# Eight buffers of split weights at eight different offsets within 512 bytes

## The chip, the cores and the metric

The kernel runs on one core of one Trainium2 chip. The metric is the time of one execution on the device in microseconds (us); where several runs are shown, it is their median. The engines are named as in the profile: PE is TensorE (PEld its weight loads), DVE is VectorE, ACT is ScalarE, POOL is GpSimd, SP is SyncE, which here only issues DMAs.

## What is computed

A trunk of two layers over 512 tokens of 1024 channels, in float32. Both layers have a token mixer and then a channel mixer with gated units, each between two RMS norms:

```python
# layer 0: retention heads and 2-D neighbourhood attention, side by side
proj = hn @ w_in
...
return jnp.concatenate([ret_out, na_out], axis=-1) @ w_out

# layer 1: bidirectional state-space mixer (SSD), 32 heads in 4 groups
proj = hn @ w_in
z, xbc, dt_raw = jnp.split(proj, [SSD_INNER, SSD_INNER + SSD_XBC], axis=-1)
xbc = jax.nn.silu(depthwise_conv_centered(xbc, conv_w, conv_b))
...
return y.astype(hn.dtype) @ w_out

# after either: up projection, convolution of width 3, gate, down projection
u = depthwise_conv_centered(hn @ w_up, conv_w, conv_b)
gate, val = jnp.split(u, 2, axis=-1)
return (jax.nn.gelu(gate, approximate=True) * val) @ w_down
```

## The kernel before

Nearly all of the work is in the weight matrices, which lie in HBM in tiles of 128 x 1024 float32. TensorE multiplies them as float32r. To keep the precision of float32, both sides of a product are split into a high part, which is the value rounded by a copy, and a low part, which is what remains. One product then takes three matmuls into the same PSUM tile (`mm3`, lines 116 to 118): high by high, low by high and high by low.

A weight tile goes through three steps. The SP queue loads it into `wst`, one of 3 buffers of 4096 bytes a partition. ScalarE copies it to `whi` (line 107) and VectorE subtracts to `wlo` (line 108), 4 buffers each:

```python
self.wst = pool("wst", 3)
self.whi = pool("whi", 4)
self.wlo = pool("wlo", 4)
```

TensorE then reads slices of 128 columns (512 bytes) of them as the stationary operand, while 512 or 256 columns of the activations `xh`, `xl` stream past (`proj_fm`), or it streams 512 columns of `whi` and `wlo` past slices of the activations (`down_tm`, the down projections, the output projections). In the rows of the profile, `mm<-xh,whi` streams `xh` over a slice of `whi`, and `mm<-whi,ab1h` streams `whi` over a slice of `ab1h`.

The feed-forward layers use Strassen's scheme: `up_strassen` makes its combined weights with `parts`, `down_strassen` with `weights`, whose activations are the tiles `axh`, `axl`, `ab1h` and `ab1l`. `mixer1` is the state-space layer. It computes the step widths first (`steps`, from a weight tile of 512 columns that is read in slices of 64), then per head a decay matrix (`head`: a row `pb` is loaded by a DMA on ACT's queue, 8 ScalarE operations on it at line 1101, an exponential into `e`), and per pair of heads the products and sums into `y`.

The order of each engine's work comes from the order of the code and from priorities (`high_priority`), with semaphores that the framework sets. The pools lie one behind the other in each partition. With `whi` and `wlo` buffers of 4096 bytes every one of the eight begins at a multiple of 512 bytes, and so do the streams `wst`, `xh`, `xl`, `H` and most work tiles. Three unused tiles do that too: "pad" in its own pool of 48 floats, and "gap" and "pad" of 32 floats each in the pool `few` of `mixer1`. Exceptions are the residual `x`, whose rows are 4224 bytes apart, and some tiles of the feed-forward layer such as `G`, `V` and `wx`, which begin at byte 480 of a block.

Of the kernel before, what the change touches and what calls it, by code (L numbers as in the profile page):

```python
# [8 lines left out]
F32 = mybir.dt.float32  # L9
R32 = mybir.dt.float32r  # L10
# [7 lines left out]
P = 128  # L18
# [12 lines left out]
class Env:  # L31
# [32 lines left out]
    def operands(self):  # L64

        self.xh, self.xl = (self.res.tile([P, KD, S], R32, name=n, tag=n) for n in ("xh", "xl"))

    def chore(self, n=1):

        for _ in range(min(n, len(self.chores))):  # L70
            self.together([self.chores.pop(0)()], [self.product])
# [9 lines left out]
    def wunit(self, src, parts=None, st=None, behind=None, low_behind=None):  # L81

        if st is None:
            st = self.wload(src)
        halves = slice(0, 512), slice(512, 1024)
        if parts is None:
            hi, lo = self.whi.tile([P, 1024], R32, name="whi"), self.wlo.tile([P, 1024], R32, name="wlo")
            with self.tc.high_priority(60):  # L90
                self.split(hi, lo, st, behind, low_behind)
            return [(hi[:, c], lo[:, c]) for c in halves]
        with nullcontext() if behind else self.tc.high_priority(60):
            for j, c in enumerate(halves):
                self.split(parts[j], parts[j + 2], st[:, c], behind)
        return [(parts[j], parts[j + 2]) for j in range(2)]
# [181 lines left out]
def down_strassen(E, big, pool, w, ts, H, first, g_post, done):  # L278
# [9 lines left out]
    def stage(i, u, cols):  # L288
        st = pool.tile([P, 1024], F32, name="wx", tag="k3") if k0[0] % 4 == 3 else E.wst.tile([P, 1024], F32, name="wst")
        k0[0] += 1  # L290
        nc.sync.dma_start(st[:, :cols], quarters(*i)[u])
        return st[:, :cols]

    def weights(i, u, extra=None):
        cols = 1024 if u < HK // 2 else 512
        st = stage(i, u, cols)
        if extra is None:
            hi, lo = E.whi.tile([P, 1024], R32, name="whi"), E.wlo.tile([P, 1024], R32, name="wlo")
        else:
            hi, lo = extra[:, :1024], extra[:, 1024:]  # L300
        with tc.high_priority(150):
            E.split(hi[:, :cols], lo[:, :cols], st)
        return [(hi[:, c:c + 512], lo[:, c:c + 512]) for c in range(0, cols, 512)]
# [34 lines left out]
    for i, (src, bank) in enumerate(seq):  # L338
# [12 lines left out]
        if last:  # L351
            ex = {4: big.tile([P, 2048], R32, name="x1", tag="s3"), 5: big.tile([P, 2048], R32, name="x2", tag="e2")}
            ws = [weights(src, u, ex.get(u)) for u in range(HK // 2 + 1)]
            for t in range(2):
                for u, x in enumerate(ws):
                    if (t, u) == (0, 1):
                        E.operands()
                    if u == 1:
                        E.finish(f"t{t}", st, done)
                    mms(t, x, u)  # L360
                E.post_half(st, 2 + t, 1, bank[t], g_post, sign=-1.0)
                E.finish(f"x{2 + t} s{2 + t}", st, done)
            continue
        for uu in ((0,), (1,), (2,), (3,), (4, 5)):
            ws = [(weights(src, u), u) for u in uu]
            for t in range(2):
                for x, u in ws:
                    mms(t, x, u)
            if uu == (1,):
                nxt = prepare(i + 1)  # L370
# [58 lines left out]
def up_strassen(E, w_up, f, X, G, V):  # L429

    nc, tc = E.nc, E.tc
    low, high = slice(0, HW), slice(HW, S)

    def load(pool, name, s, h):
        st = pool.tile([P, 1024], F32, name=name)
        nc.sync.dma_start(st.rearrange("p (f c) -> p f c", f=2),
                          w_up[s, f:f + 2, :, h * 512:h * 512 + 512].rearrange("f p c -> p f c"))
        return st  # L440

    def parts(st):
        hi, lo = E.whi.tile([P, 1024], R32, name="whi"), E.wlo.tile([P, 1024], R32, name="wlo")
        E.split(hi, lo, st)
        return hi, lo

    add = lambda o, x, y: nc.vector.tensor_tensor(o, x, y, op=ALU.add)
    q = {}

    def weights(i):  # L450
        with tc.high_priority(60):
            if i == 0:
                q[11] = load(E.wst, "wst", 0, 0)
                return parts(q[11])
            if i == 1:
                q[12], q[22] = load(E.wst, "wst", 1, 0), load(E.wst, "wst", 1, 1)
                add(q[11], q[11], q[12])
                add(q[12], q[12], q[22])
                return parts(q[12])
            if i == 2:  # L460
                q[0] = E.gain.tile([P, D], F32, name="gain")
                add(q[0], q[11], q[22])
                return parts(q[0])
            if i == 3:
                q[21] = load(E.gain, "gain", 0, 1)
                add(q[0], q[0], q[21])
                return parts(q[0])
            return parts(q[{4: 11, 5: 21, 6: 22}[i]])

    a = [E.mm.tile([P, S], F32, name="mm") for _ in range(2)]  # L470
    b, d = ([E.px.tile([P, S], F32, name="pu", tag="px") for _ in range(2)] for _ in range(2))
    order = ("A11", a), ("S3", b), ("S2", a), ("A22", b), ("R1", a), ("A12", d), ("S4", a)
    for i, (n, bank) in enumerate(order):
        hi, lo = weights(i)
        more = i in (2, 3, 4, 6)
        for j in range(2):
            for k in range(4):
                c = slice(j * 512 + k * P, j * 512 + k * P + P)
                E.mm3(bank[j][:, :HW], hi[:, c], lo[:, c], X[n][0][:, k], X[n][1][:, k], not more and k == 0, k == 3, more)
        if i == 4:  # L480
            t = E.tmp.tile([P, 2, HW], F32, name="w5", tag="tmp")
        for j in range(2):
            r = bank[j][:, :HW]
            if i in (3, 5):
                o = G[:, j, low if i == 3 else high]
                add(o, r, o)
            else:
                o = t[:, j] if i == 4 else {0: G[:, j, high], 1: V[:, j, low], 2: G[:, j, low], 6: V[:, j, high]}[i]
                nc.scalar.copy(o, r)
        if i == 4:  # L490
            add(V[:, :, low], t, V[:, :, low])
        if i in (2, 5):
            E.chore(2)
# [406 lines left out]
def mixer1(E, w_dt, w_fm, cw, dtc, cols, mask, w_out, g_post_row, done, ahead):  # L900
# [8 lines left out]
    with ExitStack() as ctx:  # L909
# [1 line left out]
        one, two, four = pool("m1", 1), pool("m1b", 2), pool("m1d", 4)  # L911

        few = pool("m1s", 1)
        few.tile([P, 32], F32, name="gap")
        few.tile([P, 32], F32, name="pad")

        cwt = few.tile([P, NG, 6, 6], F32, name="cwt")
# [18 lines left out]
        def steps():  # L936

            st = E.wst.tile([P, 512], F32, name="wst")
            nc.sync.dma_start(st, w_dt)
            wh = E.whi.tile([P, 512], R32, name="whi")  # L940
            wl = E.wlo.tile([P, 512], R32, name="wlo")
            E.split(wh, wl, st)
            ps = E.mm.tile([P, S], F32, name="mm")
            for k in range(KD):
# [286 lines left out]
        for i in range(3):  # L1231
            project(gs[0], i, p0[i])
        steps()
        ys, last, hrows, three = pool("m1y", 2), pool("m1f", 1), pool("m1p", 3), pool("m1e", 5)
        for _ in range(3):
# [49 lines left out]
def trunk(tc, x, norms, ab, ssd, ffns, out):  # L1285

    nc = tc.nc
    with ExitStack() as ctx:
# [39 lines left out]
        def ahead(w):  # L1328
            up = ffns[1][0]
            w1.extend((E.wunit(up[0, 0]), E.wunit(up[1, 0], low_behind=w), E.wload(up[0, 1])))  # L1330

        mixer1(E, *ssd, norms[1, 1], then(norms[1, 2]), ahead)
        E.chores = sums(E, ffns[1][2], ts[1])
        ffn(E, *ffns[1], ts[1], norms[1, 3], store, w1)
# [121 lines left out]
```

## Time and profile before

| | |
|---|---|
| time, median of 3 runs | 1370.81 us (1370.14 to 1371.52) |
| profiled execution | 1372.97 us, span of its instructions 1371.2 us |
| PE, PEld busy | 1344.3 us (98%), 1136.2 us (83%) |
| DVE, ACT, POOL busy | 1088.5 us (79%), 815.2 us (59%), 111.5 us (8%) |
| granted TensorE clock | 0.998 |
| DMA | 229.90 MB, mean 168 GB/s |

The profile is one execution. The span goes from its first to its last instruction; the profiled time also holds what lies around it. A record of a matmul runs from its start to its modelled end, so records of consecutive matmuls overlap: the pace is read from one start to the next. The chain of work is followed back from the last instruction to whatever released each step; a share of it is time that set the end. A group is all instructions of one line with the same tiles, with its count, busy time, the mean of one in ns, and the idle time of its engine before them.

### The profile page before, as it was taken

How to read it: one execution, taken by the hardware profiler on the slowest of the kernel's cores; microseconds unless marked ns; L12 is line 12 of the kernel's file. 1: busy time of each engine (PE TensorE's matmuls, PEld its weight loads, DVE VectorE, ACT ScalarE, POOL GpSimd, SP SyncE). 2: the span in 40 equal slices, each digit the busy share in tenths (PEclk: the TensorE clock that was granted, in tenths of full speed). 3: DMA queues.
4: the chain of work that ended last, by engine and by line, in shares of the span. 5: the costliest groups of instructions: out<-in, count | busy, mean ns of one | idle time of the engine just before them, and what ended most of it. 6: DMA issues, size and time to landing. Idle time of an engine off the chain costs nothing.

```text
span 1371.2 us, 19491 instructions
## 1 busy us (share of the span) xinstructions
PE 1344.3 (98%) x7352; PEld 1136.2 (83%) x7352; DVE 1088.5 (79%) x1524; ACT 815.2 (59%) x1345; POOL 111.5 (8%) x130
## 2 busy tenths in 40 slices
PE   7999999999999999999999999999999999999997
PEld 6877777798999888888778788787878899998886
DVE  7368878696768889697878876898789877888876
ACT  5356667453554566664878778477555455556563
POOL 1001110100111100020000110000010001110000
PEclk9999999999999999999999999999999999999999
DMA  7443232126779946654566455174433678994654
GB/s 298 144 138 99 89 100 93 49 93 218 256 210 233 250 147 193 197 201 128 142 180 194 119 178 179 48 204 110 147 128 127 224 249 214 234 242 131 196 179 145
DMA packets 73471, 229.90 MB, mean 168 GB/s; under 512 B 8352, under 2 KB 9120, under 8 KB 72864
## 3 DMA queue, kind: packets, MB, share of 16 engines
q1 hardware_dynamic: 58320, 167.30, 37.3%
q0 software_dynamic: 7168, 46.14, 13.4%
q10 hardware_dynamic: 7888, 15.21, 4.1%
q8 instruction: 58, 0.95, 0.3%
q14 instruction: 37, 0.30, 0.1%
HBM read 221.01 MB, written 51.64 MB: 199 GB/s over the span
## 4 chain that ended last, share of the span: by engine, by line
PE 83%; ACT 6%; DVE 5%; DMA 3%; issue 2%; POOL 1%; DVEq 0%; SPq 0%; POOLq 0%; ACTq 0%
PE mm L116 23%; PE mm L118 23%; PE mm L117 23%; PE pu L118 2%; PE pu L117 2%; PE pu L116 2%; PE pi L1122 1%; PE st L1071 1%; ACT pb L1101 1%; DMA pb<-pd 1%; PE py L1142 1%; ACT whi L107 1%; DVE wlo L108 1%; DMA wst<-in_c_fm 1%; PE pt L173 1%
## 5 line engine op out<-in xcount | busy, mean ns | idle before, releaser
L116 PE MATMUL mm<-xh,whi 128*128 128x512 f32 (+1 forms) x1024 | 382.5, 374 | 0.8 <-ACT z L1041 0.4
L118 PE MATMUL mm<-xl,whi 128*128 128x512 f32 (+1 forms) x1024 | 381.6, 373 | 1.0 <-DVE xl L108 0.5
L117 PE MATMUL mm<-xh,wlo 128*128 128x512 f32 (+1 forms) x1024 | 381.3, 373 | 1.0 <-DVE wlo L108 1.0
L108 DVE TENSOR_TENSOR wlo<-wst,whi 128x1024 fp32r<-128x1024 f32 (+1 forms) x232 | 280.9, 1216 | 89.9 <-ACT whi L107 88.3
L107 ACT CAST whi<-wst 128x1024 fp32r<-128x1024 f32 (+1 forms) x232 | 239.2, 1035 | 145.8 <-PE mm L117 63.5
L116 PEld LDWEIGHTS mm<-xh,whi 128*128 128x128 f32 x1024 | 192.6, 188 | 35.9 <-issue 2.3
L118 PEld LDWEIGHTS mm<-xl,whi 128*128 128x128 f32 x1024 | 192.2, 188 | 35.6 <-issue 1.3
L117 PEld LDWEIGHTS mm<-xh,wlo 128*128 128x128 f32 x1024 | 192.6, 188 | 34.2 <-DVE wlo L108 1.4
L1101 ACT ACTIVATE pb<-pb,tok 128x128 f32<-128x128 f32 x256 | 80.8, 393 | 9.3 <-DMA pb<-pd 7.9
L507 ACT ACTIVATE cv<-mm,cwt 128x512 f32<-128x512 f32 x56 | 43.5, 777 | 68.8 <-PE mm L118 68.7
L118 PE MATMUL mm<-wlo,ab1h 128*128 128x512 f32 x164 | 64.0, 390 | 0.4 <-DVE wlo L108 0.4
L116 PE MATMUL mm<-whi,ab1h 128*128 128x512 f32 x164 | 64.0, 390 | 0.0
L117 PE MATMUL mm<-whi,ab1l 128*128 128x512 f32 x164 | 63.8, 389 | 0.0
L508 DVE SCALAR_TENSOR_TENSOR cv<-mm,cwt,cv 128x511 f32<-128x511 f32 x56 | 41.7, 745 | 22.2 <-ACT cv L507 22.2
L514 ACT ACTIVATE cv<-cv 128x512 f32<-128x512 f32 x44 | 27.8, 632 | 42.8 <-DVE cv L509 42.8
L1035 DVE SCALAR_TENSOR_TENSOR xf<-mm,cwt,xf 128x511 f32<-128x511 f32 (+1 forms) x64 | 47.6, 745 | 6.2 <-ACT xf L1032 5.8
L274 POOL DMA_DIRECT2D ts<-in_f_down x48 | 30.0, 668 | 261.7 <-PE mm L118 227.7
L509 DVE SCALAR_TENSOR_TENSOR cv<-mm,cwt,cv 128x511 f32<-128x511 f32 x56 | 41.8, 746 | 0.9
L116 PE MATMUL mm<-whi,yh 128*128 128x512 f32 x104 | 40.8, 394 | 1.5 <-DVE xf L1035 1.5
L1154 POOL TENSOR_TENSOR sq<-sq 128x512 f32<-128x512 f32 x11 | 16.7, 1516 | 309.1 <-ACT sq L1148 244.6
L117 PE MATMUL mm<-whi,yl 128*128 128x512 f32 x104 | 41.1, 395 | 0.0
L116 PE MATMUL mm<-whi,xh 128*128 128x512 f32 x104 | 40.7, 398 | 0.0
(359 smaller groups left out, 2919.7 us busy)
## 6 DMA issues: line engine op xcount, KB each, us to landing
wst<-in_f_up SPq DMA_DIRECT2D x80, 512.0 KB
ts<-in_f_down POOLq DMA_DIRECT2D x48, 704.0 KB, 6.2
wst<-in_c_fm SPq DMA_DIRECT2D x40, 512.0 KB
wst<-ts SPq DMA_DIRECT2D x32, 512.0 KB
pb<-pd ACTq DMA_DIRECT2D x29, 512.0 KB
wst<-in_f_down SPq DMA_DIRECT2D x24, 512.0 KB
ts<-ts POOLq DMA_DIRECT2D x16, 704.0 KB, 9.9
wst<-in_ab_fm SPq DMA_DIRECT2D x20, 512.0 KB
```

Of the source, the lines that this page charges most:

```text
L107: first = self.nc.scalar.copy(hi, src)
L108: second = self.nc.vector.tensor_tensor(lo, src, hi.bitcast(F32), op=ALU.subtract)
L116: mm(out, lh, rh, start=first, stop=False)
L117: mm(out, ll, rh, start=False, stop=False)
L118: self.product = mm(out, lh, rl, start=False, stop=last)
L274: out.append(lambda i=i, src=src, j=j, c=c, kw=kw: gp.dma_start(part(ts, i, c), part(src, j, c), **kw))
L507: nc.scalar.activation(o, ps, AF.Identity, scale=w(1), bias=w(3))
L508: nc.vector.scalar_tensor_tensor(o[:, 1:], ps[:, :S - 1], w(0), o[:, 1:], op0=ALU.mult, op1=ALU.add)
L509: nc.vector.scalar_tensor_tensor(o[:, :S - 1], ps[:, 1:], w(2), o[:, :S - 1], op0=ALU.mult, op1=ALU.add)
L514: nc.scalar.activation(g, g, AF.Gelu_apprx_tanh)
L1035: nc.vector.scalar_tensor_tensor(r[:, a], ps[:, b], wc(j), r[:, a], op0=ALU.mult, op1=ALU.add)
L1101: nc.scalar.activation(pb[:, dr, c], pb[:, dr, c], AF.Identity, scale=1.0 - 2 * dr, bias=tok[:, 0, c, dr * H + h:dr * H + h + 1])
```

## The change

A helper `weight` takes tiles of 1040 columns (4160 bytes) from the two pools and gives out the first 1024. All places that took 1024 or 512 columns use it. The eight buffers are then 64 bytes further apart each, 512 bytes in all, and the tile "gap" of 128 bytes in `mixer1` is left out.

```diff
+    def weight(self, name):
+
+        return getattr(self, name).tile([P, 1040], R32, name=name)[:, :1024]
...
-            hi, lo = self.whi.tile([P, 1024], R32, name="whi"), self.wlo.tile([P, 1024], R32, name="wlo")
+            hi, lo = self.weight("whi"), self.weight("wlo")
...
-            hi, lo = E.whi.tile([P, 1024], R32, name="whi"), E.wlo.tile([P, 1024], R32, name="wlo")
+            hi, lo = E.weight("whi"), E.weight("wlo")
...
-        hi, lo = E.whi.tile([P, 1024], R32, name="whi"), E.wlo.tile([P, 1024], R32, name="wlo")
+        hi, lo = E.weight("whi"), E.weight("wlo")
...
         few = pool("m1s", 1)
-        few.tile([P, 32], F32, name="gap")
         few.tile([P, 32], F32, name="pad")
...
-            wh = E.whi.tile([P, 512], R32, name="whi")
-            wl = E.wlo.tile([P, 512], R32, name="wlo")
+            wh, wl = E.weight("whi")[:, :512], E.weight("wlo")[:, :512]
```

Where the tiles stand in a partition of the built programs (bytes, and the offset within a block of 512 in brackets):

```
                before                                    after
whi 0 to 3      66560  70656  74752  78848  [0 each]      66560  70720  74880  79040   [0 64 128 192]
wlo 0 to 3      82944  87040  91136  95232  [0 each]      83200  87360  91520  95680   [256 320 384 448]
gain            99328 103424                [0 each]      99840 103936                 [0 each]
y (mixer1)     200192 202240                [0 each]     200576 202624                 [384 each]
pb (mixer1)    206336 210432 214528         [0 each]     206720 210816 214912          [384 each]
```

## The prediction

> **What bounds the kernel now.** I read the page first (engines, the chain that ended last, the costliest groups), then the groups by shape, then single stretches in order of time, since a change of addresses can only be judged by how long one instruction takes.
>
> ```profile
> span 1371.2 us, 19491 instructions
> PE 1344.3 (98%) x7352; PEld 1136.2 (83%) x7352; DVE 1088.5 (79%) x1524; ACT 815.2 (59%) x1345; POOL 111.5 (8%) x130
> PE 83%; ACT 6%; DVE 5%; DMA 3%; issue 2%; POOL 1%; DVEq 0%; SPq 0%; POOLq 0%; ACTq 0%
> PE mm L116 23%; PE mm L118 23%; PE mm L117 23%; PE pu L118 2%; PE pu L117 2%; PE pu L116 2%; PE pi L1122 1%; PE st L1071 1%; ACT pb L1101 1%; DMA pb<-pd 1%; PE py L1142 1%; ACT whi L107 1%; DVE wlo L108 1%; DMA wst<-in_c_fm 1%; PE pt L173 1%
> ```
>
> TensorE is busy 98% of the span and makes 83% of the chain; three lines, the three products of every split matmul (L116 to L118), carry 69% of it. The split itself, the copy to `whi` (L107) and the subtraction to `wlo` (L108), carries 1% each. So the question is how many nanoseconds one matmul that reads a split weight takes, and whether its address has a part in that. From the timeline, TensorE alone, inside a feed-forward stretch (`whi` and `wlo` stream, the activations are the stationary side), and in the state-space layer's start:
>
> ```profile
> 539.70 0.39 PE L116 MATMUL mm<-whi,axh 128*128 128x512 f32 x1
> ...
> 541.29 0.39 PE L117 MATMUL mm<-whi,ab1l 128*128 128x512 f32 x1
> 637.62 0.28 PE L118 MATMUL mm<-xl,whi 128*128 128x256 f32 x1
> ...
> 638.10 0.39 PE L117 MATMUL mm<-xh,wlo 128*64 128x512 f32 x1
> 638.33 0.39 PE L118 MATMUL mm<-xl,whi 128*64 128x512 f32 x1
> ...
> 639.01 0.39 PE L118 MATMUL mm<-xl,whi 128*64 128x512 f32 x1
> ...
> 639.71 0.39 PE L118 MATMUL mm<-xl,whi 128*64 128x512 f32 x1
> ...
> 643.38 0.39 PE L116 MATMUL mm<-xh,whi 128*128 128x512 f32 x1
> ```
>
> The first column is the start. Between the first two rows lie 7 steps: 1.59 / 7 = 0.227 us from one 512-column matmul to the next (the 0.39 of a record is its latency, which overlaps). Between 637.62 and 638.10 lie 4 steps of 256 columns: 0.120 us each. So 256 columns more cost 0.107 us, 0.42 ns a column, and 2 x 0.120 - 0.227 = 0.013 us is a part of every matmul that doesn't grow with columns. The stream keeps this pace through a whole stretch, while the splits and the loads run beside it:
>
> ```profile
> core 0: us, PE busy (x) PEld busy (x) DVE busy (x) ACT busy (x) POOL busy (x), PEclk, DMA share, GB/s
> 505.00:545.00 40.00, 40.00 (x178) 33.13 (x177) 35.31 (x28) 25.53 (x28) 0.00 (x0) 1.00 0.50 158
> 545.00:585.00 40.00, 40.00 (x178) 33.15 (x177) 28.18 (x27) 22.81 (x29) 0.00 (x0) 1.00 0.62 200
> ```
>
> 40 us with 178 records is 0.227 us a matmul again (a record of 0.39 us counts in both stretches when it lies across the edge: 40.39 / 0.227 = 178), at granted clock 1.00, with VectorE busy for 63 of 80 us, ScalarE for 48, and the DMA engines at half their share or more. Nearly all of these streams start at byte 0 of a 512-byte block here, and they run at different speeds, so every alignment between them occurs somewhere in these 80 us; none costs a matmul anything that shows.
>
> **The change part by part.** In the built program each engine's list is the same: the same instructions, order and semaphore waits. Nothing is removed, added or moved in time, no queue sees another order, and no wait is new. What differs is addresses. (1) The eight buffers begin at bytes 0, 64, ... 448 of a 512-byte block (`whi` the lower four, `wlo` the upper four), where all began at 0. (2) Whatever lies behind them moves by 512 bytes, which keeps its offset. (3) In the state-space layer what follows the removed 128-byte "gap" (`cwt`, `col`, `bc`, `y`, `pb`, `e`, `m`) moves by 384 bytes instead; `y`, `pb`, `e` and `m` begin at 384, where they began at 0.
>
> *Matmuls.* The program has 5760 that read `whi` or `wlo` (4224 as stationary operand, 1536 as the stream); 4812 of them get a start off byte 0. What a start off 0 costs, the trace shows at one place: the 24 matmuls with 128*64 in the rows above. Their weight slices are 64 columns, 256 bytes, so that they begin at byte 0 and byte 256 by turns, three matmuls each. Their 23 steps to 643.38 take 5.28 us, 0.2296 each, 2.4 ns over the 0.227. Split by offset: the three steps into matmuls with slices at 256 take 639.01 - 638.33 = 0.68 us, the three into slices at 0 take 639.71 - 639.01 = 0.70 us. The surplus is not on the side off 0, and 0.68 / 3 is the 0.227 of the long stream. I therefore take 0. The upper end puts the whole 2.4 ns down to the offset all the same: 4812 x 2.4 ns = +11.6 us. For the lower end I look for matmuls that are now slower than the pace:
>
> ```profile
> L116 PE MATMUL mm<-xh,whi 128*128 128x512 f32 x840 | 329.6, 392 | 0.6 <-ACT z L1041 0.4 <-DVE xf L1035 0.2
> L118 PE MATMUL mm<-xl,whi 128*128 128x512 f32 x840 | 329.1, 392 | 0.0
> L117 PE MATMUL mm<-xh,wlo 128*128 128x512 f32 x840 | 328.6, 391 | 1.0 <-DVE wlo L108 1.0
> L116 PE MATMUL mm<-whi,axh 128*128 128x512 f32 x88 | 34.2, 389 | 0.0
> L117 PE MATMUL mm<-whi,yl 128*128 128x512 f32 x104 | 41.1, 395 | 0.0
> L116 PE MATMUL mm<-whi,yh 128*128 128x512 f32 x104 | 40.8, 394 | 1.5 <-DVE xf L1035 1.5
> L116 PE MATMUL mm<-whi,xh 128*128 128x512 f32 x104 | 40.7, 398 | 0.0
> ```
>
> These are groups by shape; the last number before the second bar is the mean of one in ns. The undisturbed group is at 389. If all that the others are above it were collisions of equal offsets and went away, it would be (3 + 3 + 2) x 840 = 6.7 us and (6 + 5 + 9) x 104 = 2.1 us, together -8.8 us. Against this: the group at 389 reads the same buffers at the same offsets; the others differ by standing in the mixers, where TensorE restarts after waits. So -8.8 is an end and not the value.
>
> *Splits.* 276 copies and 276 subtractions write (and the latter read) at the new offsets. Other tiles stand off 0 already. The residual `x` has rows of 4224 bytes, so its four token blocks begin at bytes 0, 128, 256 and 384, in the order of these rows (blocks 0, 1, 1, 2, 2, 3); `G` begins at byte 480, while `cv` and PSUM's `mm` are at 0:
>
> ```profile
> 6.65 1.41 DVE L164 SCALAR_TENSOR_TENSOR xs<-x,r_x,gain 128x512 f32<-128x512 f32 x2 [4.89 <-DMA gain<-in_norms]
> 9.69 0.75 DVE L164 SCALAR_TENSOR_TENSOR xs<-x,r_x,gain 128x512 f32<-128x512 f32 x1 [1.62 <-POOL r_x L146]
> 12.10 0.74 DVE L164 SCALAR_TENSOR_TENSOR xs<-x,r_x,gain 128x512 f32<-128x512 f32 x1
> 15.69 0.74 DVE L164 SCALAR_TENSOR_TENSOR xs<-x,r_x,gain 128x512 f32<-128x512 f32 x1
> 17.48 0.74 DVE L164 SCALAR_TENSOR_TENSOR xs<-x,r_x,gain 128x512 f32<-128x512 f32 x1
> 18.74 1.40 DVE L164 SCALAR_TENSOR_TENSOR xs<-x,r_x,gain 128x512 f32<-128x512 f32 x2
> L508 DVE SCALAR_TENSOR_TENSOR cv<-mm,cwt,cv 128x511 f32<-128x511 f32 x56 | 41.7, 745 | 22.2 <-ACT cv L507 22.2
> L508 DVE SCALAR_TENSOR_TENSOR cv<-G,cwt,cv 128x511 f32<-128x511 f32 x16 | 11.9, 744 | 0.0
> L107 ACT CAST whi<-wst 128x1024 fp32r<-128x1024 f32 x225 | 234.9, 1048 | 144.3 <-PE mm L117 63.1 <-DMA wst<-in_f_up 19.4 <-PE mm L118 17.1
> L108 DVE TENSOR_TENSOR wlo<-wst,whi 128x1024 fp32r<-128x1024 f32 x225 | 276.3, 1232 | 89.9 <-ACT whi L107 88.3
> ```
>
> 0.74 or 0.75 us at each offset, and 744 against 745 ns: no offset shows. I take 0. As bounds, 0.01 in 0.74 us is 1.4%, 17 ns on a subtraction and 15 on a copy; the chain's 1% each (13.7 us) is 11 subtractions and 13 copies, so +-0.4 us; the rest lies under matmuls.
>
> *The state-space tiles.* `pb` is loaded by DMA to its new place. On its queue:
>
> ```profile
> q10 hardware_dynamic: 7888, 15.21, 4.1%
>   DMA pb<-pd: 7.9, 3
> ```
>
> 4.1% of 16 engines' 1371.2 us over 7888 packets is 0.114 us for a packet of 1.93 KB; no row shows a packet at another offset. ScalarE waits three times for such a load, 7.9 us in all. [...] Without it I bound this term by the scatter of the DVE rows, 1.4% of 7.9 us: +-0.1 us. I take 0.
>
> The sum is 0, with ends of -8.8 - 0.5 = -9.3 and +11.6 + 0.5 = +12.1 us. The profiled execution took 1372.97 us (span 1371.2 and 1.8 around it), 0.16% above the median of 1370.81 of the runs, so the forecast for the median is 1370.8 us.
>
> **The rivals.** *Slower: a fetch more per matmul.* A slice off a block's start could need one more fetch at its end, which lengthens the stream or the 13 ns between streams. It decides from 2.74 us / 4812 = 0.57 ns a matmul, 1.4 columns. At four columns, 1.7 ns, it is 4812 x 1.7 = +8.2 us: 1379. For it: TensorE has no slack, any such ns lands on the end. Against it: the 0.68 us with slices at byte 256. But 256 is the kindest offset of the seven new ones, and no contiguous 512-column stream off 0 is in the trace. 0.21.
>
> *Faster: stream and weight load no longer start at the same offset.* The 13 ns per matmul could be the weight load getting in the way of the stream. If all went for 4812 matmuls, 62.6 us: 1308; for the same four columns as above, -8.2 us: 1363, and if the slower groups fell to 389 ns, 1362. Against it: at byte 256, with the stream at 0, the step is still 0.227. I give 0.17, nearly all of it to 1362 or so and 0.03 to large ones. [...]
>
> *The change does nothing to time,* since reads and writes at any multiple of 64 bytes cost alike: 1370.8, the forecast, 0.62.
>
> **How the numbers follow.** Within 0.2% (2.7 us, about what a measurement of this kernel can tell from no change), 1368.1 to 1373.5: 0.62. Slower: 0.21, faster: 0.17. The range takes in both ends of the sum, 1370.8 - 9.3 and + 12.1, so 1361 to 1383; outside it lie the large gains and losses beyond the one row that bounds them.
>
> **What would show it.** Right: 178 records in each of the two 40-us stretches, the group `mm<-whi,axh` at 389 ns and the x840 groups at 391 or 392, the splits at 1048 and 1232, the 24 matmuls in 5.3 us, the first ScalarE wait for `pb` as long as before. A slower stream would show as under 177 records there and in the steps of the 128x512 rows; a faster one as 180 and more. What makes me wrong is an effect at 64, 128 or 192 that 256 doesn't have, above all on the streaming side, where the trace has no row.

## The result and the profile after

The changed kernel took 1380.97 us in the median of 3 runs (1379.80 to 1382.41), before 1370.81: ratio 1.0075, 95% interval 1.0052 to 1.0098. In a second comparison, beside the experiments below, it took 1378.88 us against 1372.72: ratio 1.0051, interval 1.0038 to 1.0064. So it is 6 to 10 us slower.

The profiled execution took 1380.97 us with a span of 1379.2, 8.0 more than before. From its page, busy times and the chain:

```profile
span 1379.2 us, 19491 instructions
PE 1355.3 (98%) x7352; PEld 1132.9 (82%) x7352; DVE 1088.3 (79%) x1524; ACT 814.7 (59%) x1345; POOL 117.4 (9%) x130
PE 86%; DVE 5%; ACT 3%; DMA 2%; issue 2%; POOL 1%; SPq 0%; DVEq 0%; POOLq 0%; ACTq 0%
```

TensorE is busy 11.0 us longer; VectorE and ScalarE are as before. GpSimd is 5.9 us longer (111.5 before), but has 1% of the chain as before. The same two 40-us stretches as before, from the view of busy time by stretch (in brackets the number of records):

```profile
505.00:545.00 40.00, 40.00 (x175) 32.46 (x174) 34.03 (x28) 22.57 (x26) 0.00 (x0) 1.00 0.47 151
545.00:585.00 40.00, 40.00 (x174) 32.44 (x173) 29.00 (x26) 23.91 (x29) 0.00 (x0) 1.00 0.63 197
```

174 or 175 records where 178 were: the stream of 512 columns is slower while TensorE never idles, and the clock is at 1.00. But not every matmul is slower. Groups by shape:

```profile
L120 PE MATMUL mm<-xh,whi 128*128 128x512 f32 x840 | 332.6, 396 | 0.6 <-ACT z L1043 0.5
L120 PE MATMUL mm<-whi,axh 128*128 128x512 f32 x88 | 34.6, 393 | 0.0
L120 PE MATMUL mm<-xh,whi 128*128 128x256 f32 x176 | 49.3, 281 | 0.2 <-ACT xh L111 0.2
L111 ACT CAST whi<-wst 128x1024 fp32r<-128x1024 f32 x225 | 234.4, 1046 | 151.3 <-PE mm L121 69.2 <-PE mm L122 26.7 <-DMA wst<-in_f_up 13.9
L112 DVE TENSOR_TENSOR wlo<-wst,whi 128x1024 fp32r<-128x1024 f32 x225 | 275.5, 1228 | 94.4 <-ACT whi L111 87.2 <-PE pu L122 6.0
  DMA pb<-pd: 6.5, 3
```

Matmuls of 512 columns rise from 392 to 396 and from 389 to 393 ns, those of 256 columns fall from 284 to 281. The splits (1048 and 1232 before) are no slower, nor are the waits for `pb` longer (7.9 us before). The best place to see both widths is a layer's first Strassen product: 192 matmuls of 512 columns from the plain up projections are followed at once by 168 of 256 columns, with no wait between. Timeline of TensorE, start of the first of 512, of the first and of the last of 256 columns; first the kernel before, then the changed one:

```profile
299.15 0.40 PE L116 MATMUL mm<-xh,whi 128*128 128x512 f32 x1
342.70 0.28 PE L116 MATMUL mm<-xh,whi 128*128 128x256 f32 x1
362.73 0.28 PE L118 MATMUL mm<-xS,whi 128*128 128x256 f32 x1
```

```profile
301.55 0.40 PE L120 MATMUL mm<-xh,whi 128*128 128x512 f32 x1
345.83 0.28 PE L120 MATMUL mm<-xh,whi 128*128 128x256 f32 x1
365.22 0.28 PE L122 MATMUL mm<-xS,whi 128*128 128x256 f32 x1
```

Before: 43.55 / 192 = 226.8 ns and 20.03 / 167 = 119.9 ns from start to start. After: 44.28 / 192 = 230.6 and 19.39 / 167 = 116.1. The change costs 3.8 ns on each of the one kind and gains 3.8 on each of the other. The trace shows the four buffers without any address: each serves 24 of the 192 matmuls in a row, and the means of 24 steps are 233.5, 227.1, 229.2 and 232.9 ns, and the same four once more within 0.2. Before, all but the first are 226.7.

To find what decides, I took every pair of neighbouring float32r matmuls of one width in the trace of the changed kernel, and the addresses of both from the built program. The time from start to start goes by one number: the start of the *next* matmul's weight slice less the start of the stream that is running, modulo 256 bytes. I read this as the weight load that TensorE makes while the stream runs (its record begins 2 to 5 ns after the stream's, by a count in the section on why the prediction was wrong; whether the slice that is loaded counts or the one in use, the runs don't separate). (Means over pairs closer than the pace plus 25 ns, so that waits are out.)

```
difference, bytes        0       64      128      192
512 columns, ns      227.2    233.3    232.6    229.2   (0: kernel before)
256 columns, ns      119.9    114.2    118.5    114.3
```

It is the same whether the weights stand off (stream at 0, weights at 64) or the stream does (stream at 192, weights at 0, again a difference of 64: 233.2 with `whi` and `wlo` as the stream), and an offset of 256 acts as 0, 320 as 64: among the 192 matmuls above, the steps into `wlo` at 256 take 227.1 ns as those into `whi` at 0 do, and 233.6 at 320 where `whi` at 64 has 233.5. With the counts of pairs in the program (512 columns: 1009, 994, 977 at 64, 128, 192; 256 columns: 431, 434, 433) the table gives 13.5 - 5.5 = +8.0 us. I call this theory A, and tested it against others.

### The profile page after: what moved, and what is told of

Its sections match the earlier page's. It is cut to its first block, busy times and chain, and to the rows that moved or that the text cites. A ratio compares the mean times of both kernels' runs of the same rounds, so it can differ in the third digit from the quotient of the medians.

```text
span 1379.2 us, 19491 instructions
## 1 busy us (share of the span) xinstructions
PE 1355.3 (98%) x7352; PEld 1132.9 (82%) x7352; DVE 1088.3 (79%) x1524; ACT 814.7 (59%) x1345; POOL 117.4 (9%) x130
## 4 chain that ended last, share of the span: by engine, by line
PE 86%; DVE 5%; ACT 3%; DMA 2%; issue 2%; POOL 1%; SPq 0%; DVEq 0%; POOLq 0%; ACTq 0%
PE mm L120 24%; PE mm L122 23%; PE mm L121 23%; PE pu L121 2%; PE pu L122 2%; PE pu L120 2%; PE pi L1124 1%; PE st L1073 1%; DMA pb<-pd 1%; PE py L1144 1%; DMA gain<-yd 1%; PE pt L177 1%; PE pd L122 1%; PE pd L120 1%; PE pd L121 1%
```

## Experiments

The kernels share one order of instructions and waits on every engine with the kernel before; only addresses differ. Times are medians beside the kernel before on the same chip, 1372.17 us for the first four, 1372.72 for the last three.

**The moved state-space tiles alone.**

```diff
-        few.tile([P, 32], F32, name="gap")
```

> The kernel before with the 128-byte tile left out alone, so that y, pb, e and m of the state-space layer stand at byte 384 and the eight weight buffers stay at byte 0. Theory A (within TensorE, a weight load gets in the way of the stream by the difference of their addresses modulo 256): no such difference changes, so 0 us, within 1370.8 +- 2. Theory B (the moved state-space tiles and their loads carry the loss): most of the +10 us stays, and it lies between 660 and 1000 us of the span.

Measured: 1372.66 us, ratio 1.0002 (0.9994 to 1.0011). The tiles and their loads at byte 384 cost nothing that shows; theory B falls.

**All eight buffers at byte 64.** The tile "gap" is left out too, as in the run above.

```diff
         self.wst = pool("wst", 3)
+        pool("ahead", 1).tile([P, 16], F32, name="ahead")
...
         self.wlo = pool("wlo", 4)
+        pool("behind", 1).tile([P, 112], F32, name="behind")
```

> All eight weight buffers begin at byte 64 of a 512-byte block, packed as before; what lies behind them keeps its offset (the 128-byte tile is left out for the space). Theory A, with the mean steps seen after the change (512 columns: 227.2, 233.3, 232.6, 229.3 ns at a difference of 0, 64, 128, 192; 256 columns: 119.9, 114.2, 118.5, 114.3): 2485 steps of 512 columns at a difference of 64 and 1504 at 192 make +18.4 us, 1683 of 256 columns at 64 make -9.6 us, together +8.8 us: about 1379.6. Theory C (what costs is that the eight buffers have different offsets among themselves): here they are alike, so 0 us, 1370.8.

Measured: 1377.88 us, ratio 1.0039 (1.0026 to 1.0052), +5.7 us. Timeline, the same three places:

```profile
299.73 0.40 PE L118 MATMUL mm<-xh,whi 128*128 128x512 f32 x1
344.54 0.28 PE L118 MATMUL mm<-xh,whi 128*128 128x256 f32 x1
363.47 0.28 PE L120 MATMUL mm<-xS,whi 128*128 128x256 f32 x1
```

44.81 / 192 = 233.4 ns and 18.93 / 167 = 113.4 ns: the steps of a difference of 64, on every matmul of the stretch. That the buffers differ among themselves isn't needed; theory C falls. The whole is 3 us below the +8.8 of the sum; in the profile it is 2 us (+6.7), 1.5 of them in the waits, which differ by as much without a cause (see the account).

**Streams and weights moved together.**

```diff
+        pool("ahead", 1).tile([P, 16], F32, name="ahead")
         self.res = pool("res", 1)
```

> The kernel before with a tile of 64 bytes ahead of everything from the residual on: streams and weights all begin at byte 64, so that the difference between a stream and its weights is 0 as before. Theory A: 0 us, 1370.8, steps of 227 and 120 ns. Theory D (the absolute offset counts, a slice off a block's start needing one more fetch): every matmul of a split weight is off the start, at least as in the change, +8 us or more.

Measured: 1372.61 us, ratio 1.0003 (0.9994 to 1.0012). The three places:

```profile
298.23 0.40 PE L117 MATMUL mm<-xh,whi 128*128 128x512 f32 x1
341.78 0.28 PE L117 MATMUL mm<-xh,whi 128*128 128x256 f32 x1
361.81 0.28 PE L119 MATMUL mm<-xS,whi 128*128 128x256 f32 x1
```

43.55 / 192 = 226.8 and 20.03 / 167 = 119.9 ns, to the nanosecond those of before, with every buffer at byte 64. The offset as such costs nothing: theory D falls, and with it the mechanism of the prediction's slower rival.

**The other differences in steps of 16 bytes.** The edit is to the changed kernel.

```diff
-        return getattr(self, name).tile([P, 1040], R32, name=name)[:, :1024]
+        s = {"whi": 4, "wlo": 8}[name]
+        return getattr(self, name).tile([P, 1040], R32, name=name)[:, s:s + 1024]
```

> The changed kernel, with whi starting 16 and wlo 32 bytes further within its buffer: the differences between weights and stream cover all multiples of 16 modulo 256 but 0, 64, 128 and 192. Theory A, drawn straight between the four values known: the steps vary smoothly and the sum is +8.2 us, about 1379; any difference at which 512 columns take less than 227 ns or 256 columns less than 114 would make a better kernel. Theory D: every buffer is off a block's start, so no difference stands out and all are slower than 227.

Measured: 1386.51 us, ratio 1.0106 (1.0093 to 1.0119), +14.3 us. The straight line was wrong: nearly every new difference is near the worst for 512 columns. Steps by the same method, weights as the stationary side (48, 112, 176 and 240 occur only with the weights as the stream):

```
difference, bytes       16     32     80     96    144    160    208    224
512 columns, ns      232.6  232.9  232.4  233.1  232.6  234.0  233.0  227.1
256 columns, ns      118.1  118.1  119.2  117.0  117.7  117.3  118.0  117.2
```

For 512 columns only 224 is as good as 0, and nothing lies below 227; for 256 columns 64 and 192 remain the best. So 0 with 512 and 64 with 256 columns should make the best kernel of these.

**Only the weights of 256-column matmuls 64 bytes further.** Eight pools of one buffer, 4352 bytes apart, with the tags of small tiles put into the room between; `far` is set where 256 columns stream (the Strassen up products and the first units of the feed-forward and state-space layers).

```diff
+    def weight(self, name, far=False):
+
+        i = self.taken[name] % 4
+        self.taken[name] += 1
+        s = 16 if far else 0
+        return self.bufs[name][i].tile([P, 1040], R32, name=name)[:, s:s + 1024]
...
-        hi, lo = E.whi.tile([P, 1024], R32, name="whi"), E.wlo.tile([P, 1024], R32, name="wlo")
+        hi, lo = E.weight("whi", True), E.weight("wlo", True)
```

> Each weight buffer has two places, 64 bytes apart, and all eight buffers are 4352 bytes apart (the room between is filled with small tiles): weights that are read by 256-column matmuls stand at byte 64 of a 256-byte block, all others at byte 0. Theory A: 1661 steps of 256 columns at a difference of 64 gain 5.7 ns each, the 512-column steps stay at 227: -9.3 us against the kernel before, about 1362.5 where it takes 1372. If it was not the address difference but something that goes with the offset of a buffer as such, no gain.

Measured: 1366.55 us against 1372.72, ratio 0.9955 (0.9942 to 0.9967), -6.2 us: faster than both kernels, but 3 us short of the -9.3 expected. The three places:

```profile
297.72 0.39 PE L130 MATMUL mm<-xh,whi 128*128 128x512 f32 x1
341.26 0.28 PE L130 MATMUL mm<-xh,whi 128*128 128x256 f32 x1
360.59 0.28 PE L132 MATMUL mm<-xS,whi 128*128 128x256 f32 x1
```

43.54 / 192 = 226.8 ns as before, 19.33 / 167 = 115.7 ns instead of 119.9. It gets less than the 113.4 of all eight at 64. One of the seven products (S2) has its stream 64 bytes further too, by a neighbour that grew, so its difference is 0 and its step 120.0. The two products ahead of it (A11 and S3) took 117.8 at a difference of 64, and the four behind it 113.3 to 114.2.

So the address difference alone does not set the pace at 256 columns: at 64 there are two steady ones. The state-space layer of this run shows both on one weight tile, the third unit, which two passes read against the two halves of `xh`. The rows are the first and the last of 21 neighbouring matmuls in either pass, and between them a matmul of 512 columns that comes in early in the second pass:

```profile
620.37 0.28 PE L130 MATMUL mm<-xh,whi 128*128 128x256 f32 x1
622.73 0.28 PE L132 MATMUL mm<-xl,whi 128*128 128x256 f32 x1
624.93 0.40 PE L130 MATMUL mm<-xh,whi 128*64 128x512 f32 x1
630.29 0.28 PE L130 MATMUL mm<-xh,whi 128*128 128x256 f32 x1
632.55 0.28 PE L132 MATMUL mm<-xl,whi 128*128 128x256 f32 x1
```

2.36 / 20 = 118 ns in the first pass, 2.26 / 20 = 113 in the second, at the same difference of 64. The half of `xh` isn't it: against that of the first pass the first two units ran at 113.3. The pace changed only where other matmuls came between, eight transposes ahead of the third unit and the one of 512 columns in the second pass. With all eight buffers at 64, A11 and S3 ran at 113.5 and 113.3. So S3 is no exception of its own: A11 ahead of it already has its pace. What chooses the pace no run shows; the steps of 256 columns in the tables are means over both. A11, S3 and S2, 24 matmuls each in eight places, at 113.3 in place of 117.8, 117.8 and 120.0 would be 3.0 us, an estimate of what is left to gain there.

**The other way round: only those of 512 columns further.** Against the run above; the extra weight tiles of the feed-forward layer's first units, 64 bytes further there, stay at byte 0 here.

```diff
-        s = 16 if far else 0
+        s = 0 if far else 16
```

> The same layout the other way round: only weights read or streamed by 512-column matmuls stand 64 bytes further, those of 256 columns stay at byte 0. Theory A: 2475 steps at a difference of 64 cost 6.1 ns and 1505 at 192 cost 2.1 ns: +18.2 us, about 1390 where the kernel before takes 1372. The sum of this and the other one is that of all eight buffers at byte 64.

Measured: 1388.87 us, ratio 1.0118 (1.0105 to 1.0131), +16.2 us. The three places:

```profile
301.90 0.40 PE L130 MATMUL mm<-xh,whi 128*128 128x512 f32 x1
346.70 0.28 PE L130 MATMUL mm<-xh,whi 128*128 128x256 f32 x1
366.72 0.28 PE L132 MATMUL mm<-xS,whi 128*128 128x256 f32 x1
```

44.80 / 192 = 233.3 and 20.02 / 167 = 119.9 ns: this time the loss alone, 2 us under the 18.2 expected. The two runs were expected to add up to that of all eight buffers at 64; they make -6.2 + 16.2 = +10.0 us, not +5.7. By the account below 2.2 us of the gap are steps of 256 columns (-7.9 in place of -10.1), where the pace isn't a matter of the difference alone.

**The change once more.**

> The changed kernel once more, beside the two others on one chip. Theory A, from the steps and their counts: +8.2 us.

Measured: 1378.88 us, +6.2, ratio 1.0051 (1.0038 to 1.0064). The sum's +8.0 us is 0.58%, inside this interval and that of the first comparison.

**The account.** For each trace, all starts of TensorE's matmuls, less those of the kernel before (us). "Steps" are what start-to-start times are over 226.67 and 120 ns by up to 25 ns, "waits" what is over that, "other" the matmuls that aren't float32r.

```
                      512 steps  256 steps   waits   other    sum   span
the change              +15.6       -5.6      -1.9    -0.1   +8.0   +8.0
all eight at 64         +18.4      -10.1      -1.5     0.0   +6.8   +6.7
steps of 16             +19.9       -3.2      -1.4    -1.0  +14.3  +14.3
256 columns alone        +0.2       -7.9      -1.2    +0.6   -8.3   -8.4
512 columns alone       +18.4       -0.2      -0.4    -1.6  +16.2  +16.1
```

The steps carry it. In the change they make +10.0 us, and the waits give 1.9 back. Single executions differ by about as much: in the first and third experiments, where no step changed, the waits are 0.8 and 1.1 us shorter than in the trace of before, and in the profile of the last run 3.8, with steps of +15.4 and -5.6. So the agreement of the table's +8.0 with the span's +8.0 is partly luck; its 512-column term is 2 us too small. What the slower TensorE does bring is more time for the splits: ScalarE waits longer for TensorE (its idle time before line 111 that TensorE ended is 69.2 + 26.7 us, before it was 63.1 + 17.1).

## Why the prediction was wrong

**The step that failed** is the first term, 4812 matmuls off byte 0, which I took as 0. It was +15.6 us for 512 columns and -5.6 for 256 by the account (13.5 and 5.5 by the table). Three parts of its working failed.

The row that I put nearest, the 24 matmuls of the step widths, had slices at byte 256. By the table 256 is 0, so that row could not show the effect. The text called 256 the kindest of the offsets, which for 512 columns it is in the changed kernel (227.1 ns among the 192 matmuls above, 229.0 to 233.8 at the others), and kept the value all the same. The block is a poor stand-in besides: its slices are 64 columns, and in the changed kernel, at a difference of 128, it runs from 641.71 to 646.99, 5.28 us for 23 steps as before (why these steps are 229.6 ns and not 226.7 at a difference of 0, no run shows):

```profile
641.71 0.40 PE L121 MATMUL mm<-xh,wlo 128*64 128x512 f32 x1
646.99 0.39 PE L120 MATMUL mm<-xh,whi 128*128 128x512 f32 x1
```

The second part was the even pace over 80 us, from which I concluded that every alignment occurs and none costs anything. That can hold for ScalarE, VectorE and the DMAs: over these 80 us in the trace of before, their instructions and packets begin 3 to 214, 23 to 220 and 0 to 226 ns after the start of the matmul that runs. A weight load runs at a fixed time against the stream of its own engine (in the trace of before, 5926 of 5941 steps without a wait have the next load's record begin 2 to 5 ns after the running stream's), so with all buffers at 0 only one alignment of these two ever occurred, and an even pace is what a constant loss looks like, too.

The third was the 13 ns that don't grow with columns. The faster rival named them as a collision of weight load and stream at equal offsets, which could go. With 256 columns a part of them can go: 5.7 ns at a difference of 64, and 6.5 in the cleanest stretch (113.4 in place of 119.9). With 512 columns equal offsets are the best found, and the same shift costs 6.1 ns. Of the steps between two matmuls that read split weights, with no wait in either trace, 3892 are of 512 columns (+15.1 us in all) and 1661 of 256 (-5.6), so the sign of the sum is that of the larger group. I had no row for two widths reacting in opposite ways, and the rival took one sign for all.

**The rule under the forecast**, that reads and writes at any multiple of 64 bytes cost alike, was my assumption; no row showed it. With 512 columns the step is 227.2 ns at a difference of 0 and 233.3, 232.6 and 229.2 at 64, 128 and 192.

**The slower rival** had the right sign and order of size (1379) but the wrong mechanism: the streams and weights moved together would have been slower by it, and were not. It decided from 0.57 ns a matmul; the mean over the 4812 was 8.0 us / 4812 = 1.7 ns, by chance the value that I had put in for four columns.

**What held.** Splits: 1046 and 1228 ns, the term 0 within 0.4 us. State-space tiles: 0, by the first experiment alone; the packets of queue 10, which are all of `pb`, took 4.1% of 16 engines' span before and after, and 4.2% in that experiment. The bound of 0.1 us on this term came from the scatter of VectorE's rows alone. No new order and no new wait. The range, 1361 to 1383, held the time, since it took in ends that I did not believe. The check named for it worked: under 177 records in the 40-us stretches.

With the same stream and weight load, a matmul of 512 columns takes 226.8 or 233.4 ns by the difference of their addresses alone (the third and the second experiment). Whether that lies in the memory or in something within TensorE, no run here shows.

## What to carry to other kernels

Where TensorE has no slack, look at the start address of each weight slice against that of the stream running while it loads, modulo 256 bytes, and choose it per matmul width: here equal offsets for 512 columns (227.2 ns, 233.3 at 64), 64 or 192 apart for 256 (114.2 and 114.3 ns, 119.9 at 0), in float32r. For 256 columns read the pace from the trace all the same, since one difference ran at 113.3 and at 117.8. Judge a change of addresses by whether the trace holds the alignment in question at all: a weight load and the stream of the same engine kept their relation here for the whole run (2 to 5 ns in 5926 of 5941 steps), so an even pace says nothing of other relations. A row that stands in for a missing one has to differ in the very quantity that changes, and 256 did not differ from 0 (227.1 ns both).

## What the runs showed of the hardware

- The step from one 128 x 512 float32r matmul to the next is 226.7 ns at best and 234.0 at worst of the 16-byte differences tried, that of 128 x 256 is 113.3 at best and 119.9 at a difference of 0. No mean over a difference that was tried is below 226.7 for 512 columns.
- An offset of 256 acts as 0 (227.1 ns both) and 320 as 64 (233.6 and 233.5), and the effect goes by the difference, not by either address: all at byte 64 runs to the nanosecond as all at byte 0 (226.8 and 119.9 ns).
- At 256 columns and a difference of 64 there are two steady paces, 113.3 and 117.8 ns; the same weight tile ran at both.
- ScalarE and VectorE did not react to offsets of 64 to 448 bytes (splits of 1046 and 1228 ns against 1048 and 1232), nor did the loads of `pb` to byte 384 (ratio of the kernel 1.0002).
- Open: why the two widths prefer opposite differences, what chooses between the two paces at 256 columns, and what differences that are no multiples of 16 bytes do.
